# A residual block on one core: another order of the last pair of gate columns, earlier loads for the attention stage, and the meta tokens' probabilities transposed first

## The chip, the core and the metric

The kernel runs on one core of one Trainium2 chip. Its engines are PE (TensorE, the matrix unit), DVE (VectorE), ACT (ScalarE), POOL (GpSimd) and SP, which here only issues DMAs. Each engine works through its own instructions strictly in the order in which they were written, and waits for the others by semaphores. DMAs are issued from two queues: SP's (the weights) and POOL's (most stores and loads of activations, between POOL's own arithmetic). The metric is the device time of one execution in microseconds (us), from the first to the last instruction with what lies around it.

## The reference

One layer over 512 tokens and 16 prepended meta tokens (528 rows), width 2048, all in float32:

```
h = rmsnorm(r, mix_pre_g)
z = h @ w_in + b_in                    # q | k | v | forget logits | pool input u | g_attn | g_pool
c = cumsum(log_sigmoid(f_logit))       # per head
s = q @ k.T * 128**-0.5 + c[q] - c[k]  # causal, 8 heads of 128
attn = softmax(s) @ v
d = trailing_mean(u, windows 2,4,8,16) - u
pool = (d @ pool_w per group) * pool_scale
m = sigmoid(g_attn) * (attn @ w_attn_o) + sigmoid(g_pool) * (pool @ w_pool_o)
r = r + rmsnorm(m @ w_out, mix_post_g)
h = rmsnorm(r, ffn_pre_g)
a = causal_dwconv3(h @ w_ffn_up)
r = r + rmsnorm((gelu(gate(a)) * val(a)) @ w_ffn_down, ffn_post_g)
out = r[16:]
```

## The kernel before

Activations are kept transposed, 128 features in the partitions and the 528 tokens along the free axis. Every float32 product is made of three matmuls in the fast float32r format: both operands are split into a high part (a cast on ACT, line 292 or 193) and a low part (a subtraction on DVE, line 293 or 201), and `mm3` (line 303) adds high*high, high*low and low*high in PSUM.

**Input projection.** After four single columns the other 60 column blocks of `w_in` go through in pairs, in the order of `xpairs`. A pair is one step of Strassen's scheme (`strassen`): seven products of 24 matmuls each instead of eight. Its left factors are halves of the weights ("11", "12", "22") and sums of them ("S1" to "S4"); its right factors are blocks of x ("11", "21", "22", held in the tiles `xb`, `xh`, `xl`) and sums of them ("T1" to "T4", held in `ht`, `lt`). Products add up in the PSUM banks `pua`, `pub`, `puc`; ACT copies them out (lines 491 to 505) and DVE adds them. The list `units` (line 134) says in which order the weights' halves and sums are prepared, some three units ahead of PE.

**Work in the background.** `side` and `side2` hold generators. After each k of `mm3` they get a tick of that k's matmul time, and when the time that a generator asked for with `yield` is over, its next piece is written into the program there. So the background's place in the program is set by the amount of matmul work, not by what has finished. The output of a pair (`x_out`) goes this way: multiply by `rstd` on DVE (line 574), bias or sigmoid on ACT (line 578), store to DRAM from POOL (line 582).

**Between the pairs and the next projections.** The pool differences d come back from DRAM into eight tiles (`d_loads`, line 595, on SP's queue), are split into `dh` and `dl`, and `pool_out` multiplies them with the pool weights: four groups g, two outputs each, 24 matmuls a group, into the banks `py`, copied out as `yh` (ACT, line 796) and `yl` (DVE, line 797). After group 0, `forget_columns` loads the cumulated forget values (`fc`, line 469) and transposes them on PE (`pc`, line 472), and `head_loads` loads q, k and v of heads 0 and 1.

**po and attention.** Sixteen blocks of the pool's output projection follow (`half_proj`, banks `ppo`, 48 matmuls each); their results are multiplied by the gates (line 844) and stored (line 845). During them two lanes run in the background: lane 0 has heads 0, 2, 4, 6, lane 1 has heads 1, 3, 5, 7. For a head, `head_parts` splits q and k, transposes v (`pv`, `pvm`) and makes the products of the last two meta queries (`p2`, line 669). `attention` then goes through four blocks of 128 queries (i = 3, 2, 1, 0): bias row `dd` from the broadcast forget row `crow` (ACT, line 685), mask (POOL, line 686), scores `ps` (PE, line 691), then `s`, maximum, exponential (lines 695 to 699). Then the probabilities are transposed, key block by key block (`pt`, line 716, j = 3, 2, 1, 0) and split into `pth` and `ptl`; the 16 meta keys' probabilities are transposed last (`pm`, line 731) and split into `pmh`; and `pa` (line 742) multiplies with v: first the meta tokens, then j = 0, 1, 2, 3. At the end of lane 1 stand the meta tokens' own queries (`meta_queries`, lines 748 to 775). After that the attention's output projection (`pao`) begins.

All F tiles (activations) share one pool of 63 buffers that are handed out again when the last reader of a tile has run; PSUM has eight banks (tag "s") that go round, so a new bank waits for the copy-out of the tile that held it. The DMAs of POOL's queue use eight semaphores in turn; a DMA that takes one up again waits until the DMA that had it has landed.

Of the kernel before, what the change touches and what calls it, by code (L numbers as in the profile page):

```python
# [23 lines left out]
F32 = mybir.dt.float32  # L24
# [25 lines left out]
H = 8  # L50
# [24 lines left out]
def block(ctx, tc, xT, win, wf, wao, wpw, wpo, wout, wup, wdn, consts, out):  # L75
# [50 lines left out]

    loads, units, base = [], [], []
    for key in order:
        base.append(len(units))
        if key[0] == "pair":  # L130
            at0 = len(loads)
            for src in key[1:]:
                loads += [(srcs[src[0]](src[1]), c) for c in (0, 1024)]
            units += [(i, at0) for i in ("11", "12", "S2", "S1", "S3", "S4", "22")]
        else:
            for c in (0, 1024):
                units.append(("", len(loads)))
                loads.append((srcs[key[0]](*key[1:]), c))
# [29 lines left out]
    def make_source():  # L168
        i = at["sum"]
        kind, n = units[i]  # L170
        if kind == "":
            sources[i] = raw_of(n)
        else:
            a11, a12, a21, a22 = (raw_of(n + j) for j in range(4))
            if kind == "S2":
                for name in ("S1", "S2"):
                    sums[name] = wp.tile([P, 1024], F32, name="wsum", tag="wsum", bufs=2)
                dve.tensor_tensor(sums["S1"], a21, a22, op=OP.add)
                dve.tensor_tensor(sums["S2"], sums["S1"], a11, op=OP.subtract)  # L179
            elif kind == "S3":  # L180
                dve.tensor_tensor(a21, a11, a21, op=OP.subtract)
                drop(n)
            elif kind == "S4":
                dve.tensor_tensor(a12, a12, sums["S2"], op=OP.subtract)  # L184
            sources[i] = {"11": a11, "12": a12, "S3": a21, "S4": a12, "22": a22}.get(kind) or sums[kind]
# [281 lines left out]
    def forget_columns():  # L467
        cur = F("fc")[:H]
        nc.gpsimd.dma_start(cur, c_dram)
# [9 lines left out]
    def strassen(keys, blocks, n, skip=0, late=None):  # L479
# [26 lines left out]
        dve.tensor_tensor(gr, gr, c[:, skip:], op=OP.add)  # L506
        return zg, zv
# [91 lines left out]
    ds = []  # L599
# [20 lines left out]
    for ma, mb in xpairs:  # L620
        last = (ma, mb) == xpairs[-1]
# [52 lines left out]
    def attention(h, then=None):  # L674
# [36 lines left out]

        pth = [None] * 4
# [88 lines left out]
    for j, t in enumerate(ds):  # L801
        dh[j], dl[j] = F("dh", F32R), F("dl", F32R)
        split(t[:, T0:], dh[j][:, T0:], dl[j][:, T0:])
    ds.clear()

    def lane(n):
        if n:
            yield 8.0
# [19 lines left out]
    sg = {}  # L828
# [8 lines left out]
    for j in range(KT):  # L837
# [7 lines left out]
        nc.gpsimd.dma_start(po_dram[j][:, T0:], t[:, T0:])  # L845
    side.finish()
# [4 lines left out]
    pl = {}  # L851

    def sum_load(j):
        if j < KT:
            gate_load(j)
            pl[j] = F("pl")
            nc.gpsimd.dma_start(pl[j][:, T0:], po_dram[j][:, T0:])

    sum_load(0)
    sum_load(1)  # L860
# [354 lines left out]
```

## Time and profile before

| | |
|---|---|
| runs of the kernel before | median 2671.09 us of 3 (2663.85 to 2672.19) |
| the profiled execution | 2668.45 us, of which the span from the first to the last instruction is 2666.6 us |
| busy in the span | PE 96%, PE weight loads 92%, DVE 73%, ACT 45%, POOL 9% |
| PE's mean granted clock | 0.981 of full speed |

The share of busy time is a mean over stages with different limits. "PEclk" in a window is the granted clock: 1.00 is the upper of its two levels, 0.50 the lower, and values between are a mixture of the two in that window. A matmul's duration overlaps with the next, so PE's busy time has no gap where matmuls follow each other.

### The profile page before, as it was taken

The page shows a single profiled execution, that of the slowest core. Times are in us where ns is not written, and L with a number is a line of the kernel's source. Part 1 is how long each engine was busy: PE and PEld are TensorE (multiplying, and loading weights), DVE is VectorE, ACT ScalarE, POOL GpSimd, SP SyncE. Part 2 cuts the span into 40 slices and gives each one's busy share as a digit, 9 for nine tenths or more (in the row PEclk, how much of TensorE's full clock was granted, in tenths as well). Part 3 has the DMA queues.
Part 4 walks back from the last instruction along what each step waited for, and adds up shares of the span by engine and source line. Part 5 has one row for each costly group of instructions (what it writes and reads, how often), then busy time and mean ns, then how long its engine had stood idle before and what let it go on. Part 6 is the DMA issues. An engine that isn't in the chain of part 4 may idle for free.

```text
span 2666.6 us, 46374 instructions
## 1 busy us (share of the span) xinstructions
PE 2558.5 (96%) x18949; PEld 2450.8 (92%) x18949; DVE 1937.9 (73%) x2542; ACT 1210.7 (45%) x1851; POOL 227.2 (9%) x369
## 2 busy tenths in 40 slices
PE   8899999999888999999899999999999999999995
PEld 7899999999878899999899999999999978888885
DVE  8887778778766653489798888888888844545456
ACT  5544444444544423455555555455555542222232
POOL 3000000000122210034000000000000000000003
PEclk9999999999998999999999999999999999999997
DMA  4333433343543453578753333333333343333323
GB/s 165 104 121 135 139 125 122 134 143 121 200 141 113 137 179 99 181 243 274 225 182 125 110 115 124 119 107 123 127 108 119 125 155 113 122 116 122 114 90 127
DMA packets 129269, 369.57 MB, mean 139 GB/s; under 512 B 15758, under 2 KB 42128, under 8 KB 129056
## 3 DMA queue, kind: packets, MB, share of 16 engines
q1 hardware_dynamic: 112064, 310.48, 35.7%
q0 software_dynamic: 16992, 56.14, 5.7%
q8 instruction: 148, 2.42, 0.4%
q14 instruction: 65, 0.53, 0.1%
HBM read 319.34 MB, written 47.21 MB: 137 GB/s over the span
## 4 chain that ended last, share of the span: by engine, by line
PE 82%; DVE 7%; issue 6%; DMA 2%; ACT 2%; POOL 1%; SPq 0%; POOLq 0%; DVEq 0%; ACTq 0%
PE pua L303 28%; PE pd L303 18%; PE puc L303 14%; PE pub L303 7%; PE pw L303 6%; PE pu L303 4%; PE pao L303 3%; DVE wlo L201 1%; PE ppo L303 1%; PE pa L742 1%; DMA t<-h_dram 1%; ACT whi L193 1%; DVE xb L370 0%; DVE xr L543 0%; DVE lt L524 0%
## 5 line engine op out<-in xcount | busy, mean ns | idle before, releaser
L201 DVE TENSOR_TENSOR wlo<-wraw,whi 128x1024 fp32r<-128x1024 f32 x566 | 696.8, 1235 | 216.9 <-ACT whi L193 216.7
L193 ACT CAST whi<-wraw 128x1024 fp32r<-128x1024 f32 x566 | 594.3, 1051 | 517.6 <-DVE wraw L184 176.4
L303 PE MATMUL pua<-lt,whi 128*128 128x258 f32 (+1 forms) x1632 | 464.1, 284 | 0.0
L303 PE MATMUL pua<-h,whi 128*128 128x258 f32 x1520 | 371.0, 284 | 5.1 <-ACT z L491 5.1
L303 PE MATMUL pua<-h,wlo 128*128 128x258 f32 x1216 | 344.4, 283 | 0.0
L303 PEld LDWEIGHTS pua<-lt,whi 128*128 128x128 f32 x1632 | 309.9, 190 | 0.0
L303 PEld LDWEIGHTS pua<-h,whi 128*128 128x128 f32 x1520 | 267.4, 190 | 5.3 <-ACT z L491 5.3
L193 ACT CAST whi<-wsum 128x1024 fp32r<-128x1024 f32 x136 | 142.9, 1051 | 255.8 <-DVE wsum L179 251.7
L303 PE MATMUL pd<-fl,whi 128*128 128x512 f32 x640 | 252.1, 394 | 1.1 <-DVE fl L293 1.1
L303 PE MATMUL pd<-fh,wlo 128*128 128x512 f32 x640 | 251.7, 393 | 0.0
L303 PE MATMUL pd<-fh,whi 128*128 128x512 f32 x640 | 251.2, 393 | 0.0
L303 PEld LDWEIGHTS pua<-h,wlo 128*128 128x128 f32 x1216 | 231.4, 190 | 0.0
L1072 DVE TENSOR_TENSOR yacc<-yacc,pd 128x512 f32<-128x512 f32 x144 | 98.8, 686 | 167.6 <-PE pd L303 167.5
L303 PE MATMUL pua<-ht,whi 128*128 128x264 f32 x720 | 206.0, 286 | 12.2 <-ACT z L491 10.1
L303 PE MATMUL pua<-ht,wlo 128*128 128x264 f32 x720 | 205.2, 285 | 0.0
L201 DVE TENSOR_TENSOR wlo<-wsum,whi 128x1024 fp32r<-128x1024 f32 x136 | 166.0, 1222 | 53.9 <-ACT whi L193 53.9
L303 PE MATMUL puc<-h,whi 128*128 128x258 f32 x912 | 196.2, 282 | 0.0
L303 PE MATMUL puc<-h,wlo 128*128 128x258 f32 x608 | 171.4, 282 | 0.0
L303 PE MATMUL puc<-lt,whi 128*128 128x258 f32 (+1 forms) x544 | 153.9, 283 | 0.0
L303 PEld LDWEIGHTS puc<-h,whi 128*128 128x128 f32 x912 | 151.3, 189 | 0.0
L303 PEld LDWEIGHTS pua<-ht,whi 128*128 128x128 f32 x720 | 136.4, 189 | 12.8 <-ACT z L491 10.3
L303 PEld LDWEIGHTS pd<-fl,whi 128*128 128x128 f32 x640 | 120.1, 188 | 30.2 <-DVE fl L293 2.3
(326 smaller groups left out, 6305.4 us busy)
## 6 DMA issues: line engine op xcount, KB each, us to landing
wraw<-wup SPq DMA_DIRECT2D x200, 512.0 KB, 3.8
wraw<-win SPq DMA_DIRECT2D x128, 512.0 KB, 4.0
wraw<-wdn SPq DMA_DIRECT2D x88, 512.0 KB, 3.6
wraw<-wout SPq DMA_DIRECT2D x56, 512.0 KB, 4.4
act_dram<-cv POOLq DMA_DIRECT2D x44, 256.0 KB, 5.0
y<-act_dram SPq DMA_DIRECT2D x44, 256.0 KB, 4.9
sig_dram<-z POOLq DMA_DIRECT2D x32, 264.0 KB, 4.5
sg<-sig_dram POOLq DMA_DIRECT2D x32, 264.0 KB, 4.2
```

Source lines behind the costliest of these rows:

```text
L193: act.copy(ready[i][0], sources[i])
L201: dve.tensor_tensor(lo, sources.pop(i), f32(ready[i][0]), op=OP.subtract)
L303: pe.matmul(po, a, b[:, xs], start=k == 0 and j == 0 and not more, stop=k == nk - 1 and j == 2, skip_group_check=more)
L742: pe.matmul(pa[:, q0:], u, w, start=n == 0 and j == 0, stop=n == 4 and j == 2)
L1072: dve.tensor_tensor(yacc[i], yacc[i], ps, op=OP.add)
```

## The change

- The last pair takes a new function, `strassen_early`, and its weights the order EARLY. The three products that read x itself (right factors "21", "11", "22") come first, the four that read the sums after them. It uses a fourth PSUM bank (`pud`) and no `snap` copy; products five and six (T3, T4) both add to `pua`.
- A generator `prefetch` takes the place of `d_loads`: after the third product it loads `fc`, the eight d tiles and q, k, v of heads 0 and 1, all from POOL's queue.
- The d tiles are split four ahead of group 0, two after group 0, and two after group 1. Head 0's parts are added to the background after group 0 instead of group 2, and lane 1 begins after 4.0 us of matmul time instead of 8.0.
- The pairs' loop now stands behind the definitions of the attention; the output of the last pair is written out in the background's flush behind the first four d splits.
- In `attention` the meta keys are transposed and split first, ahead of the four key blocks, and `pa` takes the meta tokens, then j = 3, 2, 1, 0.
- The first two loads of the po results (`sum_load`) are issued within the po loop.

```
+    LATE = ("11", "12", "S2", "S1", "S3", "S4", "22")
+    EARLY = ("12", "11", "S4", "S2", "S1", "S3", "22")
...
-            units += [(i, at0) for i in ("11", "12", "S2", "S1", "S3", "S4", "22")]
+            early = key == ("pair", ("in", xpairs[-1][0]), ("in", xpairs[-1][1]))
+            units += [(i, at0) for i in (EARLY if early else LATE)]
...
-    def forget_columns():
-        cur = F("fc")[:H]
-        nc.gpsimd.dma_start(cur, c_dram)
+    def forget_columns(cur):
...
+    def strassen_early(keys, blocks, n, late):
+
+        unit = pair_weights(*keys)
+        a, b, c, d = (s_ps(x)[:, :n] for x in ("pua", "pub", "puc", "pud"))
+        zg, zv = F("z"), F("z")
...
+        gl, gr, vl, vr = zg[:, :n], zg[:, n:2 * n], zv[:, :n], zv[:, n:2 * n]
+        product(0, b, "21")
+        product(1, a, "11")
+        act.copy(gl, a)
+        product(2, d, "22")
+        side.add(late)
+        dve.tensor_tensor(gl, gl, b, op=OP.add)
+        product(3, a, "T2", True)
+        act.copy(gr, a)
+        product(4, c, "T1")
+        dve.tensor_tensor(gr, gr, d, op=OP.add)
+        product(5, a, "T3", True)
+        act.copy(vr, a)
+        dve.tensor_tensor(gr, gr, c, op=OP.add)
+        product(6, a, "T4", True)
+        act.copy(vl, a)
+        dve.tensor_tensor(vr, vr, c, op=OP.add)
+        return zg, zv
...
-    def d_loads():
-        for j in range(8):
-            t = F("d")
-            nc.sync.dma_start(t[:, T0:], d_dram[j][:, T0:])
-            ds.append(t)
-        yield 0.1
...
-        za, zb = strassen((("in", ma), ("in", mb)), XBLOCKS, XN, late=d_loads() if last else None)
-        side.add(x_out((ma, za), (mb, zb)))
-    side.finish()
-    side2.finish()
...
+        pm = s_ps("pm")
+        for i in range(4):
+            pe.transpose(pm[:META, P * i:P * (i + 1)], probs[i][0][:, :META], ident)
+        m = wp.tile([P, 1024], F32R, name="pmh", tag="wsum", bufs=2)[:META]
+        split(pm[:META], m[:, :512], m[:, 512:])
+        yield 1.2
         pth = [None] * 4
         for j in (3, 2, 1, 0):
...
-        pm = s_ps("pm")
-        for i in range(4):
-            pe.transpose(pm[:META, P * i:P * (i + 1)], probs[i][0][:, :META], ident)
-        m = wp.tile([P, 1024], F32R, name="pmh", tag="wsum", bufs=2)[:META]
-        split(pm[:META], m[:, :512], m[:, 512:])
-        yield 2.5
+        yield 1.3
...
-        for j in range(4):
+        for j in (3, 2, 1, 0):
             c = slice(P * j, P * (j + 1))
             steps.append((vh[:, c], vl[:, c], *pth[j], min(P * j, 256)))
...
+    def prefetch():
+
+        ds.append(F("fc"))
+        nc.gpsimd.dma_start(ds[0][:H], c_dram)
+        for j in range(8):
+            ds.append(F("d"))
+            nc.gpsimd.dma_start(ds[-1][:, T0:], d_dram[j][:, T0:])
+        head_loads(0)
+        head_loads(1)
+        yield 0.1
...
+        if last:
+            za, zb = strassen_early(keys, XBLOCKS, XN, prefetch())
...
+        if last:
+            side.finish()
+            side2.finish()
+        side.add(x_out((ma, za), (mb, zb)))
...
+    for j in range(4):
+        d_split(j)
+    side.finish()
...
-            yield 8.0
+            yield 4.0
...
         if g == 0:
-            forget_columns()
-            head_loads(0)
-            head_loads(1)
-        if g == 2:
+            forget_columns(fc)
+            del fc
             side.add(head_parts(0))
+        if g < 2:
+            d_split(2 * g + 4)
+            d_split(2 * g + 5)
...
+        if j == KT - 2:
+            sum_load(0)
+            sum_load(1)
```

On POOL, around the end of the last pair, the order of issues was this before (`sig_dram<-z` are the stores of the gates, `sg` the gates' loads for po):

```order
L582 DMA sig_dram<-z 128x528 x8
L469 DMA fc<-c_dram 8x528
L646 DMA qkv<-qkv_dram 128x528 x6
L833 DMA sg<-sig_dram 128x528 x2
L634 DMA crow<-c_dram 128x528
L646 DMA qkv<-qkv_dram 128x528 x3
L686 AFFINE_SELECT dd<-dd 128x128 x2
L833 DMA sg<-sig_dram 128x528
L845 DMA po_dram<-sg 128x514
L634 DMA crow<-c_dram 128x528 x2
```

And now:

```order
L611 DMA sig_dram<-z 128x528 x6
L819 DMA fc<-c_dram 8x528
L822 DMA d<-d_dram 128x514 x8
L660 DMA qkv<-qkv_dram 128x528 x6
L611 DMA sig_dram<-z 128x528 x2
L648 DMA crow<-c_dram 128x528
L885 DMA sg<-sig_dram 128x528 x2
L700 AFFINE_SELECT dd<-dd 128x128 x4
L885 DMA sg<-sig_dram 128x528
L897 DMA po_dram<-sg 128x514
L648 DMA crow<-c_dram 128x528
```

The fifteen loads have moved ahead of the last pair's own two stores, the d loads came over from SP's queue, and heads 1 and 2 no longer have their `crow` loads together behind the second po store: head 1's stands behind the first.

On ACT, at the end of the last pair, before:

```order
L505 COPY z<-pua 128x264
L578 ACTIVATE z<-z,cs 128x528 x2
L292 CAST dh<-d 128x514 x8
L796 ACTIVATE yh<-py,cs 128x258
L796 ACTIVATE yh<-py,cs 128x256
```

And now:

```order
L534 COPY z<-pua 128x264
L295 CAST dh<-d 128x514 x4
L607 ACTIVATE z<-z,cs 128x528 x2
L811 ACTIVATE yh<-py,cs 128x258
L811 ACTIVATE yh<-py,cs 128x256
L295 CAST dh<-d 128x514 x2
L295 CAST qh<-qkv 128x528
L295 CAST vh<-pv 128x512
L295 CAST vmh<-pvm 16x128
```

Four splits of d now come ahead of the last pair's output, and its two activations stand between them and the copies out of group 0; head 0's parts stand between the copies out of group 0 and those of group 1.

On PE, in head 0 (rows of `ppo` and `ps` between them are left out here), before:

```order
L716 MATMUL pt<-ident,s 128x128 x4
L731 MATMUL pm<-ident,s 16x128 x4
L742 MATMUL pa<-pmh,vmh 128x512 x2
L742 MATMUL pa<-pth,vh 128x512
L742 MATMUL pa<-pth,vh 128x384
L742 MATMUL pa<-pth,vh 128x256 x2
```

And now:

```order
L728 MATMUL pm<-ident,s 16x128 x4
L736 MATMUL pt<-ident,s 128x128
L736 MATMUL pt<-ident,s 128x128 x4
L757 MATMUL pa<-pmh,vmh 128x512 x2
L757 MATMUL pa<-pth,vh 128x256 x2
L757 MATMUL pa<-pth,vh 128x384
L757 MATMUL pa<-pth,vh 128x512
```

The transposes of the meta keys have moved ahead of all those of the key blocks, and within `pa` the block that is transposed last (j = 0, 512 columns) is now the last to be read.

## Rows read from the trace of the kernel before

**Rows 1.** Windows of 100 and 50 us: each engine's busy time, granted clock, DMA share.

```profile
core 0: us, PE busy (x) PEld busy (x) DVE busy (x) ACT busy (x) POOL busy (x), PEclk, DMA share, GB/s
500.00:600.00 100.00, 100.00 (x822) 100.00 (x821) 78.65 (x87) 49.68 (x70) 5.42 (x10) 1.00 0.39 132
700.00:750.00 50.00, 41.10 (x318) 39.95 (x317) 33.60 (x71) 31.40 (x62) 11.98 (x23) 0.93 0.63 223
750.00:800.00 50.00, 39.88 (x267) 36.00 (x267) 32.01 (x84) 19.78 (x47) 13.91 (x32) 0.91 0.49 150
800.00:850.00 50.00, 45.92 (x308) 42.70 (x307) 33.22 (x84) 23.36 (x55) 12.38 (x31) 0.88 0.43 128
850.00:900.00 50.00, 44.73 (x310) 40.47 (x309) 33.67 (x85) 23.07 (x55) 8.72 (x23) 0.93 0.24 77
```

**Rows 2.** PE's waits, 640 to 960 us: total, times, longest.

```profile
PE ppo L303 <- DVE s L695: 4.8, 2, 3.6
PE pa L742 <- DVE pmh L293: 4.8, 7, 1.2
PE pc L472 <- DMA fc<-c_dram: 4.1, 1, 4.1
PE p L669 <- DVE vl L293: 4.0, 3, 2.1
PE pa L742 <- ACT pmh L292: 3.3, 4, 1.4
PE py L303 <- ACT dh L292: 2.5, 1, 2.5
PE ps L691 <- DVE pth L293: 1.4, 1, 1.4
...
PE pua L303 <- ACT z L496: 0.8, 1, 0.8
PE pt L766 <- DVE s L758: 0.7, 1, 0.7
...
PE pa L775 <- DVE vm L772: 0.4, 1, 0.4
```

**Rows 3.** Windows of 5 us, same columns as Rows 1.

```profile
715.00:720.00 5.00, 2.06 (x12) 2.02 (x13) 2.57 (x7) 2.71 (x6) 2.62 (x5) 0.62 1.03 413
...
815.00:820.00 5.00, 4.85 (x15) 3.91 (x16) 3.89 (x13) 1.44 (x3) 2.72 (x5) 0.52 0.42 124
```

**Rows 4.** Timeline of PE: start, us, line, operation, out<-in, idle before and its releaser.

```profile
814.31 0.50 PE L742 MATMUL pa<-pmh,vmh 16*128 16x512 f32 x1 [1.13 <-ACT pmh L292]
```

**Rows 5.** Timeline of ACT and DVE, 707 to 720 us.

```profile
707.76 0.38 ACT L505 COPY z<-pua 128x264 f32<-128x264 f32 x1 [2.02 <-PE pua L303]
708.11 1.53 ACT L578 ACTIVATE z<-z,cs 128x528 f32<-128x528 f32 x2
...
711.74 2.59 ACT L292 CAST dh<-d 128x514 fp32r<-128x514 f32 x4 [0.81 <-DMA d<-d_dram]
...
707.37 1.51 DVE L574 TENSOR_TENSOR z<-z,rstd 128x528 f32<-128x528 f32 x2
...
712.39 2.66 DVE L293 TENSOR_TENSOR dl<-d,dh 128x514 fp32r<-128x514 f32 x4 [0.74 <-ACT dh L292]
```

**Rows 6.** Timeline of POOL's and SP's queues: start, us, operation, count, idle before.

```profile
701.22 0.54 POOL L582 DMA_DIRECT2D sig_dram<-z  x1 [2.37 <-ACT z L578]
...
710.47 0.52 POOL L469 DMA_DIRECT2D fc<-c_dram  x1
...
752.60 0.55 POOL L845 DMA_DIRECT2D po_dram<-sg  x1 [7.63 <-DVE sg L844]
...
705.05 4.10 SPq L595 DMA_DIRECT2D d<-d_dram  x8
```

**Rows 7.** Tile qkv: time from issue to landing of its loads.

```profile
DMA to landing us min/median/max: 3.1/6.0/8.2
```

**Rows 8.** The chain of waits, 640 to 960 us: start, us, what.

```profile
771.71 2.85 PE pa L742 x14
```

More of the change, by code (lines that the diff above doesn't have):

```diff
@@ L174, in make_source @@
             a11, a12, a21, a22 = (raw_of(n + j) for j in range(4))
-            if kind == "S2":
+            if kind in ("S2", "S4") and (n, "S2") not in sums:
                 for name in ("S1", "S2"):
[L177 to L180, printed above, removed]
+                    sums[n, name] = wp.tile([P, 1024], F32, name="wsum", tag="wsum", bufs=2)
+                dve.tensor_tensor(sums[n, "S1"], a21, a22, op=OP.add)
+                dve.tensor_tensor(sums[n, "S2"], sums[n, "S1"], a11, op=OP.subtract)
+            if kind == "S3":
                 dve.tensor_tensor(a21, a11, a21, op=OP.subtract)
@@ L183, in make_source @@
             elif kind == "S4":
-                dve.tensor_tensor(a12, a12, sums["S2"], op=OP.subtract)
-            sources[i] = {"11": a11, "12": a12, "S3": a21, "S4": a12, "22": a22}.get(kind) or sums[kind]
+                dve.tensor_tensor(a12, a12, sums[n, "S2"], op=OP.subtract)
+            sources[i] = {"11": a11, "12": a12, "S3": a21, "S4": a12, "22": a22}.get(kind) or sums[n, kind]
         at["sum"] += 1
@@ L506, in strassen, with product @@
         dve.tensor_tensor(gr, gr, c[:, skip:], op=OP.add)
+        return zg, zv
[3 more added lines that the diff above has]
+        zg, zv = F("z"), F("z")
+        def product(i, ps, block, more=False):
+            mm3([(ps, slice(0, n))], HK, unit(i), blocks[block], more)
+        gl, gr, vl, vr = zg[:, :n], zg[:, n:2 * n], zv[:, :n], zv[:, n:2 * n]
[15 more added lines that the diff above has]
+        dve.tensor_tensor(vr, vr, c, op=OP.add)
         return zg, zv
@@ L590, in x_evac @@
         side.add(x_out((m, z), scaled=True))
-    def d_loads():
-        for j in range(8):
-            t = F("d")
-            nc.sync.dma_start(t[:, T0:], d_dram[j][:, T0:])
-            ds.append(t)
-        yield 0.1
-    ds = []
     XBLOCKS = {"11": lambda k: xb[0, k], "21": lambda k: xb[0, HK + k], "22": lambda k: xb[1, HK + k]}
@@ L619, in block @@
     side2.add(forget())
-    for ma, mb in xpairs:
-        last = (ma, mb) == xpairs[-1]
-        za, zb = strassen((("in", ma), ("in", mb)), XBLOCKS, XN, late=d_loads() if last else None)
-        side.add(x_out((ma, za), (mb, zb)))
-    side.finish()
-    side2.finish()
     vmeta = cp.tile([P, H, META], F32, name="vmeta")
@@ L799, in pool_out, with d_split @@
             yl.append(lo)
-    for j, t in enumerate(ds):
-        dh[j], dl[j] = F("dh", F32R), F("dl", F32R)
-        split(t[:, T0:], dh[j][:, T0:], dl[j][:, T0:])
-    ds.clear()
+    def prefetch():
[7 more added lines that the diff above has]
+        yield 0.1
+    ds = []
+    for ma, mb in xpairs:
+        last = (ma, mb) == xpairs[-1]
+        keys = ("in", ma), ("in", mb)
+        if last:
+            za, zb = strassen_early(keys, XBLOCKS, XN, prefetch())
+        else:
+            za, zb = strassen(keys, XBLOCKS, XN)
+        if last:
+            side.finish()
+            side2.finish()
+        side.add(x_out((ma, za), (mb, zb)))
+    fc = ds.pop(0)[:H]
+    def d_split(j):
+        dh[j], dl[j] = F("dh", F32R), F("dl", F32R)
+        split(ds[j][:, T0:], dh[j][:, T0:], dl[j][:, T0:])
+        ds[j] = None
+    for j in range(4):
+        d_split(j)
+    side.finish()
     def lane(n):
         if n:
-            yield 8.0
+            yield 4.0
             yield from head_parts(n)
@@ L827, in block, with sum_load @@
     po_dram = dp.tile([KT, P, L], F32, name="po_dram")
-    sg = {}
+    sg, pl = {}, {}
+    def sum_load(j):
+        if j < KT:
+            gate_load(j)
+            pl[j] = F("pl")
+            nc.gpsimd.dma_start(pl[j][:, T0:], po_dram[j][:, T0:])
     def gate_load(n):
@@ L850, in block @@
     mh, ml = [], []
[L851 to L860, printed above, removed]
     for j in range(KT):
```

## The prediction

> **What bounds the kernel now.** I read the windows first, to see where PE is not full. Over most of the program PE is busy without a gap at full clock, 822 matmuls in 100 us, or 0.122 us each; in the stretch from 700 to 900 us, pool projection and attention, it is busy 41 + 40 + 46 + 45 of 200 us and its clock is 0.93, 0.91, 0.88, 0.93 [rows 1]. Elsewhere in the program this change alters nothing on PE, so its whole worth must come from this stretch. It loses time in two ways. PE stands still for 28.4 us in the four windows [rows 1]. And it runs at the lower of its two clock levels: a window at clock c has (1 - c) / 0.5 of its time at half pace, so 7 + 9 + 12 + 7 = 35 us [rows 1]. Half of that, 17.5 us, is lost if PE has work all through; it has not in the window from 715 us, where it is busy 2.06 of 5 us, so I count 14 us.
>
> Next, PE's waits say what for. In groups: the start of the pool projection 6.6 us (2.5 for the first split of d, 4.1 for the forget row fc); `pa` for the split of the meta keys 8.1 us (4.8 + 3.3); `ppo` and `ps` at the start of the attention lanes for `s` and `pth` 6.2 us (4.8 + 1.4); the meta queries' product `p2` for the split of v 4.0 us; the end of lane 1 1.1 us (0.7 + 0.4) [rows 2]. DVE and ACT are no bound here: DVE is busy about 33 of each 50 us, ACT 20 to 31 [rows 1]. These are latencies of chains across engines. Last, where the low clock sits: 0.62 in the window in which PE waits for fc, and 0.52 in the one from 815 us, in which PE gets through 15 matmuls [rows 3] and which begins with `pa` behind a wait of 1.13 us for the split of the meta keys [rows 4].
>
> **The change part by part.** The terms are made against the profiled execution, 2668.45 us; the median of the three runs is 2.6 us above it.
>
> *Order of the last pair.* The same 168 matmuls. New is that T4 adds to `pua` right behind T3, with ACT's copy out between them, so PE waits for that copy. The trace has a wait of this kind, `pua` for the copy of line 496: 0.8 us [rows 2]; I take **+0.8**, between 0.5 (the copy alone is 0.38 [rows 5]) and 1.9 (a weight cast ahead of it on ACT). One ACT copy is dropped, one DVE add is added, and the weight sum S4 is needed one product after its operands; that lies under a product's 24 x 0.122 = 2.9 us, several of which are prepared ahead: 0.
>
> *First split of d.* Before, PE waited 2.5 us for `dh`, since ACT did the last copy, then two activations of 1.53 us in all [rows 5], and the d loads could only be issued from 705.05 us, behind weight loads on SP's queue [rows 6]. Now the prefetch stands behind the store of the pair before, issued at 701.22 us [rows 6], and each issue takes 0.54, so the first d is asked for at about 702.3, 2.8 us earlier, and ACT goes from the last copy straight to the split. What is late next: copy 0.38, one split 2.59 / 4 = 0.65, some 0.2 between, then 0.5 of the low part (2.66 / 4 = 0.67, PE has two matmuls meanwhile) [rows 5]: 1.7 against 2.5. **-0.8**; from -2 to +2 if d lands late.
>
> *fc.* It was issued at 710.47 [rows 6], now some 8.6 us earlier and ahead of the other loads. Even with the DMA engines as full as they were then (share 1.03 [rows 3]) that is more than twice the wait. **-4.1**, and 0 to lose.
>
> *New waits within the pool projection.* Head 0's parts now sit in group 1. `pv` takes the bank of the first `py`, which is free when DVE has made `yl`. PE gets there 24 + 5 + 6 matmuls after the first `py`, 4.3 us. ACT and DVE first finish four d splits (DVE 2.66), then DVE multiplies the last pair's output by rstd (1.51), ACT does its second activation (0.75), then `yh` and `yl`, some 0.45 each [rows 5]: 5.8 us. So 1.5 us of wait, 0.4 more for `pvm`. In group 2 the same again, a bank behind the split of v (0.7), and a bank behind `yl` and a weight split (0.5). Together 3.1, **+3.0**. The lower bound is 0. For the upper, q, k and v must have landed: v of head 0 is the third load behind the d loads, asked for at about 709.5, and these loads took 3.1 to 8.2 us [rows 7], so it lands up to 717.7 against PE at about 715: up to +5.5.
>
> *The meta keys first.* Between `pm` and the first `pa` matmul stood some 18 matmuls of `ppo`, 18 x 0.122 = 2.2 us, and the waits of 8.1 us over eight heads say that this was 1 us too little on average. Now `pmh` is ready four transposes earlier. What is late next is `ptl` of block j = 0. Its distance to `pa` is again 12 to 18 matmuls, but `pa` reads it last: behind twelve matmuls at 2.85 / 14 = 0.20 us [rows 8], 2.4 us more. That is more than the mean wait of 1.0 and about the longest sum of one head (1.4 + 1.2 [rows 2]). **-7.5**, from -8.1 to -4 (half of it back where DVE is late).
>
> *Start of the lanes.* `ppo` waited 3.6 us because head 1's `crow` load stood on POOL behind the second po store, which had itself waited 7.63 us for DVE [rows 6]. It now stands behind the first. But the load itself still has to land before DVE can go on, so I take **-2.0** of the 5.0 (3.6 + 1.4); from -5 to 0. `p2` still waits for the split of v as before: **0**.
>
> *End.* The meta queries now have po matmuls beside them: **-1.1**. The early po result loads save nothing, as PE has no wait for them.
>
> *Clock.* Of the 35 us at half pace, the stretches behind `pa` waits are about half; the pool projection's may return, since its new waits sum to nearly what the old were. Of 14 us lost I take a third, **-5.0**, from -14 to 0.
>
> Sum: 0.8 - 0.8 - 4.1 + 3.0 - 7.5 - 2.0 - 1.1 - 5.0 = -16.7, so 2668.45 - 16.7 = 2651.75; I forecast 2651.8.
>
> **The rivals.**
> *The clock stays low.* The long waits are cut up into short ones at bank changes, and the half-pace time stays at 35 us. For it: the window at 0.52 follows a wait of 1.13 us, and no wait of `pa` is longer than 1.4 [rows 2 to 4]. Against it: their number falls. Without the clock term 2668.45 - 11.7 = 2656.8. The Trainium skill ("TensorE: Matmul & The Clock Gate", section "A second HAM failure mode: psum-queue depth-cycling") says that a PE which idles briefly and often between groups of matmuls, as PSUM banks are cycled, swings between its two clock levels though no single pause is long. By that rule this rival would hold; the trace agrees in so far as that low window follows a short wait.
> *The waits only move.* With eight banks and DVE in order, `pa` then waits for block 0 or the next bank instead: 2 of the 8.1 are gained, start and clock give nothing: 0.8 - 0.8 - 4.1 + 3.0 - 2.0 - 1.1 = -4.2, 2664.2. For it: `ppo` and `pvm` already wait for DVE today. Against: DVE is a third idle.
> *All of it comes.* No new waits in the pool projection, the start's 5.0, `pa`'s 8.1 and the clock's 14: 0.8 - 0.8 - 4.1 - 8.1 - 5.0 - 1.1 - 14 = -32.3, 2636.2.
> *Slower, by POOL's queue.* Each later head's `crow` and q, k, v loads come to stand behind a po store that waits for DVE, as head 1's did. Each such head costs 3.6 + 1.4 and a stretch at half pace, some 2.7: 7.7 us. From three heads on it eats the gain; with four, and the start's 2.0 not gained, 2651.8 + 31 + 2 = 2685. For it: the queue is in order and now carries eight loads more. Against: these eight are over before po begins, and before only one head was hit.
>
> **How the numbers follow.** Forecast 0.51, clock stays low 0.17, all of it 0.10, waits only move 0.14, slower 0.08. A difference under 0.3%, 8 us, cannot be told from none. The first three are faster by more: 0.78. Waits that only move are within it: 0.14. Slower: 0.08. The likeliest case alone spans 2642 to 2660 (the clock term by 5 either way, the `pa` and pool terms by 3 each). The range goes from 2637, next to the case in which all comes, to 2667, past that in which waits move; outside are the slower case and about a half of the full gain.
>
> **What would show it.** PE's wait for fc gone; first `py` within 1.5 us of the last pair's end; PE's waits for `pmh` under 1 us in all and none of more than 1 us for `ptl` of block 0; a new wait of `pv` or `pvm` for `yl` of 1 to 2 us; `pao` beginning some 17 us earlier, with the program behind it unchanged; the stretch's half-pace time about 25 us. The prediction is wrong if the clock falls in the pool projection for longer than before, if `pv` waits for its load well past 718 us, or if `crow` is late for more than one head.

## The result and the profile after

The changed kernel took 2652.94 us, median of 4 runs (2649.82 to 2655.38), against 2669.00 us, median of 4, for the kernel before: ratio 0.9939, 95% interval 0.9926 to 0.9952, 16.1 us less. Forecast were 2651.8 us in a range of 2637 to 2667. The profiled execution took 2654.53 us, span 2652.8 us.

The same windows of the changed kernel as in [rows 1] (us; each engine's busy time with its instructions; granted clock; DMA share; GB/s):

```profile
500.00:600.00 100.00, 100.00 (x822) 100.00 (x821) 80.30 (x88) 48.33 (x68) 5.04 (x10) 1.00 0.37 125
700.00:750.00 50.00, 43.00 (x325) 41.57 (x324) 35.99 (x78) 31.31 (x62) 17.78 (x35) 0.93 0.64 222
750.00:800.00 50.00, 44.85 (x316) 40.87 (x315) 34.62 (x89) 24.80 (x57) 13.53 (x34) 0.93 0.50 159
800.00:850.00 50.00, 47.28 (x335) 43.15 (x336) 39.13 (x104) 26.19 (x62) 12.97 (x32) 0.97 0.42 130
850.00:900.00 50.00, 45.54 (x345) 42.13 (x344) 31.46 (x77) 20.75 (x46) 8.29 (x23) 1.00 0.35 111
```

In the window from 500 us, ahead of the stretch, nothing has changed: 822 matmuls, as before. Inside the stretch PE's busy time has gone from 171.6 to 180.7 of 200 us, and the time at half pace, (1 - clock) / 0.5 of each window, from 35 to 7 + 7 + 3 + 0 = 17 us.

The stage can be cut out of the trace by PE's own first rows: from the first matmul of the last pair to the first `pao`. Before, it ran from 687.07 to 921.64, 234.57 us; after, from 689.14 to 906.98, 217.84 us. These are the first `pao` rows of before and of after (start, us, what, idle before):

```profile
921.64 0.51 PE L303 MATMUL pao<-ah,whi 128*128 128x258 f32 x2 [0.25 <-ACT ah L292]
```
```profile
906.98 0.51 PE L306 MATMUL pao<-ah,whi 128*128 128x258 f32 x2 [0.25 <-ACT ah L295]
```

So the stage is 16.73 us shorter. The program ahead of it took 2.07 us longer and the program behind it 0.86 us (1744.96 and 1745.82 us to the end of the span), so the two profiled executions differ by 13.8 us in all. By the first `ppo` matmul the stage divides into the pair with the pool projection, 42.64 before and 40.65 after (-1.99), and the lanes, 191.93 and 177.19 (-14.74). PE's idle times in its timeline add up to 29.55 us before (28 of them) and 19.12 after (21); the other 6.3 us are time in which PE works, now with about half as much of it at half pace.

PE's waits after, 640 to 960 us (total, times, longest), which answer to [rows 2]:

```profile
PE pt L736 <- DVE pmh L296: 3.5, 3, 1.6
PE pv L674 <- DMA qkv<-qkv_dram: 2.9, 1, 2.9
PE pvm L677 <- DVE vl L296: 2.4, 1, 2.4
PE ps L705 <- DVE s L709: 1.6, 1, 1.6
PE pm L728 <- DVE s L653: 1.5, 1, 1.5
PE pv L674 <- DVE ptl L296: 1.2, 1, 1.2
PE py L306 <- ACT dh L295: 1.0, 1, 1.0
PE pa L757 <- ACT pth L295: 0.9, 1, 0.9
...
PE pa L757 <- DVE ptl L296: 0.7, 2, 0.5
PE ppo L306 <- DVE pmh L296: 0.7, 1, 0.7
```

The wait for `fc` is gone, and `pa`, which waited 8.1 us for the meta keys, waits 0.9 + 0.7. New are `pt` behind `pmh` (a transpose that needs a PSUM bank which DVE has not yet read), `pv` behind its own load, and `pvm` behind the split of `v`.

### The profile page after: what moved, and what is told of

The parts are those of the page before. It is cut to its first block, busy times and chain, and to the rows that moved or that the text cites. A ratio compares the mean times of both kernels' runs of the same rounds, so it can differ in the third digit from the quotient of the medians.

```text
span 2652.8 us, 46370 instructions
## 1 busy us (share of the span) xinstructions
PE 2555.4 (96%) x18949; PEld 2447.4 (92%) x18949; DVE 1934.3 (73%) x2543; ACT 1209.4 (46%) x1850; POOL 230.1 (9%) x377
## 4 chain that ended last, share of the span: by engine, by line
PE 61%; DVE 3%; issue 3%; DMA 2%; POOL 1%; ACT 1%; SPq 0%; POOLq 0%; DVEq 0%; ACTq 0%
PE pd L306 18%; PE pua L306 16%; PE puc L306 8%; PE pw L306 6%; PE pub L306 4%; PE pao L306 3%; PE pu L306 3%; PE ppo L306 1%; DVE wlo L204 1%; PE pa L757 0%; DMA t<-h_dram 0%; DMA x<-xT 0%; POOL mix L973 0%; PE ps_rs L324 0%; DVE mix L969 0%
## 5 line engine op out<-in xcount | busy, mean ns | idle before, releaser
L306 PEld LDWEIGHTS pua<-ht,whi 128*128 128x128 f32 x720 | 136.6, 190 | 12.9 <-ACT z L492 10.4
```

The lines of the kernel that those rows point to most:

```text
L306: pe.matmul(po, a, b[:, xs], start=k == 0 and j == 0 and not more, stop=k == nk - 1 and j == 2, skip_group_check=more)
```

## The experiments

All medians, with the range of the runs, the ratio to the kernel before on the same chip, and the stage in one profiled execution each (first matmul of the last pair to first `ppo`; first `ppo` to first `pao`). In the first column "loads" is the new order of the last pair with the earlier loads, "meta" the meta keys first, "lane 4" the odd lane at a pace of 4 instead of 8.

| kernel | us (runs) | ratio [95%] | pool part | lanes |
|---|---|---|---|---|
| before | 2667.8 to 2669.0 in five sets | | 42.6 | 191.9 |
| lane 4 | 2675.0 (2672.7 to 2678.0) | 1.0029 [1.0018, 1.0040] | 41.4 | 199.5 |
| meta | 2658.1 (2656.4 to 2660.4) | 0.9962 [0.9950, 0.9975] | 41.6 | 182.6 |
| loads | 2659.4 (2656.4 to 2661.7) | 0.9971 [0.9960, 0.9981] | 40.4 | 184.1 |
| meta + lane 4 | 2660.8 (2656.2 to 2662.2) | 0.9972 [0.9963, 0.9981] | 43.1 | 183.2 |
| loads + lane 4 | 2662.2 (2660.8 to 2665.4) | 0.9974 [0.9965, 0.9984] | 40.6 | 190.7 |
| loads + meta | 2659.5 (2656.1 to 2660.6) | 0.9963 [0.9951, 0.9976] | 41.2 | 183.6 |
| all three (the change), again | 2653.6 (2650.4 to 2656.9) | 0.9951 [0.9938, 0.9963] | 41.7 | 178.8 |
| change, odd lane at 2 | 2656.3 (2654.0 to 2656.6) | 0.9952 [0.9939, 0.9964] | 40.7 | 179.1 |
| change, old order of the pair | 2649.6 (2646.8 to 2650.5) | 0.9928 [0.9915, 0.9940] | 40.7 | 177.5 |
| change, head 0 ahead of d4 | 2647.0 (2646.2 to 2648.9) | 0.9928 [0.9915, 0.9940] | 38.9 | 178.2 |
| that, old order of the pair | 2648.4 (2644.6 to 2649.2) | 0.9921 [0.9907, 0.9934] | 38.5 | 177.7 |
| that, head 1's `crow` early | 2648.7 (2645.9 to 2649.0) | 0.9923 [0.9909, 0.9936] | 39.1 | 176.7 |

How far single executions scatter: the changed kernel's two profiles have 217.84 and 220.49 us in the stage.

### The parts of the change, one at a time and in pairs

**Meta first, alone.** `pm` and its split ahead of the four blocks, and the accumulation turned round, in the kernel before:

```diff
+        pm = s_ps("pm")
...
+        yield 1.2
         pth = [None] * 4
         for j in (3, 2, 1, 0):
...
-        yield 2.5
+        yield 1.3
         pa = s_ps("pa")
...
-        for j in range(4):
+        for j in (3, 2, 1, 0):
```

> The kernel before with one part of the change: the meta tokens' probabilities are transposed, copied and subtracted ahead of the four key blocks instead of behind them, and the output's accumulation goes m, 3, 2, 1, 0 instead of m, 0, 1, 2, 3. Theory (the prediction's own term): the 14 waits of the output for ACT's and DVE's copies, 8.1 us in all, go nearly whole, so 7.5 us less than before and a little clock with it: about 2660 us, the stage from the first matmul of the last pair to the first one of the attention projection 8 to 10 us shorter. Rival (the waits only move: transposes of the blocks wait for PSUM banks behind the meta tokens' split, as 3.5 us of pt's waits in the changed kernel hint): 0 to 2 us less, about 2668 us, and the gain of the whole change lies in the earlier loads.

2658.1 us, 10.7 us less than before; the stage is 10.4 us shorter, 9.3 of them in the lanes. The theory has the number, and `pa`'s waits go as it said: 8.1 us before, 0.4 now. But the rival is right about the waits: 5.6 us of waits for `pmh` have come up at other places, and these are the three largest (PE's waits of this kernel; total, times, longest):

```profile
PE ps L691 <- DVE pmh L293: 2.2, 1, 2.2
PE pvm L663 <- DVE pmh L293: 1.6, 1, 1.6
PE pt L722 <- DVE pmh L293: 1.3, 1, 1.3
```

PE's idle time in the lanes is 20.7 us, against 22.8 before, so only 2.0 of the 9.3 us are idle time. The other 7.3 are time in which PE works, at a mean granted clock of 0.96 over the lanes instead of 0.93. Why the clock was higher is not shown.

**All but the meta keys.** The same lines put back in the changed kernel.

> The changed kernel with the meta tokens' probabilities put back behind the four blocks and the old order of the output's accumulation; the new order of the last pair, the early loads and the start of the lanes stay. Theory: the output waits again as it did, 7 to 8 us, so 2660 us, about half of the change's 16 us; fc's wait stays away. Rival (waits only move): 2653 to 2655 us, no measurable difference from the changed kernel.

2662.2 us, 9.3 us above the first set of the changed kernel and 8.6 above the second. `pa`'s waits are back, 15.1 us in four groups, of which these two are the largest (PE's waits of this kernel, total, times, longest):

```profile
PE pa L756 <- ACT pmh L295: 8.2, 4, 3.3
PE pa L756 <- DVE pmh L296: 5.1, 7, 1.8
```

**The odd lane at 8 again.** In the changed kernel:

```diff
-            yield 4.0
+            yield 8.0
             yield from head_parts(n)
```

> The changed kernel with the odd heads' lane starting after a pace of 8 instead of 4 (as before). Theory (the prediction's term for the start of the lanes, which gave it 2.0 us): the second lane's first head comes later and the first half of the first two projection blocks has less work to put between its waits: 1 to 3 us more, 2654 to 2656 us. Rival: the first waits of the odd lane (2.4 us for the split of v, 1.6 us for s) come from its starting too early, while its row of c still loads behind the first store of the pool projection; with 8 they are hidden and the time is 1 to 3 us less, 2650 to 2652 us.

2659.5 us: 6 to 7 us lost, more than either theory gave to this one number. The rows show a wait that neither the kernel before nor the changed one has, that of the meta queries' product `p` (L683) for ACT's copy of k. PE's waits (total, times, longest), and PE's and ACT's timelines at one of the three places:

```profile
PE p L683 <- ACT kh L295: 8.5, 3, 4.0
```
```profile
819.23 0.60 PE L674 MATMUL pv<-ident,qkv 128*128 128x128 f32 x4
823.16 0.38 PE L683 MATMUL p<-kh,qh 128*128 128x256 f32 x1 [3.22 <-ACT kh L295]
```
```profile
821.44 0.52 ACT L713 ACTIVATE s<-s,st 128x272 f32<-128x272 f32 x1 [1.97 <-DVE st L652]
821.87 0.19 ACT L713 ACTIVATION_READ_ACCUMULATOR s<-s,st 128x1 f32 x1
821.96 0.61 ACT L295 CAST qh<-qkv 128x528 fp32r<-128x528 f32 x1
822.48 0.63 ACT L295 CAST kh<-qkv 128x528 fp32r<-128x528 f32 x1
```

The next head's q and k were there, but in ACT's order their split stands behind the other lane's exponential, and this waited 1.97 us for DVE's `st` (the row names line 652, a reciprocal; the maximum of these scores, lines 711 and 712, ends just before it). PE has passed `pv` at 819.23 and stands before the meta queries' product until 823.16. The wait is set by which lane's work is ahead of which in an in-order engine.

**The loads alone** (the changed kernel with meta last and the odd lane at 8), **meta first with lane 4** (the kernel before with these two edits), and **lane 4 alone**:

> The changed kernel with the meta tokens last again and the odd lane starting after a pace of 8 again: what is left of the change are the order of the last pair and the earlier loads. Theory (the prediction's terms for these: fc 4.1 and the first split 0.8 us less, T4's wait 0.8 and the wait of v's transposes 3.0 us more, a microsecond or so of clock): about 2667 us, 1 to 3 us less than before. Rival (each part simply adds: with meta first and the odd lane at 4 worth 9.3 and 6.6 us, nothing is left for the loads): 2669 us, as before. A second rival (the loads carry the gain, since they let the lanes begin 10 us earlier): 2660 us or less.

> The kernel before with two parts of the change, the meta tokens first and the odd lane at a pace of 4, with the old order and the old loads. Theory: the gain in the stage of the lanes doesn't need the earlier loads, so all of the change but the 2 us by which its pool projection ended sooner: 2654 to 2656 us. Rival: the early start of the odd lane pays only once its q, k and v are there; with the old loads its first head waits for them, and the time stays at the 2658 us of the meta tokens alone, or above.

> The kernel before with one part of the change, the odd lane starting after a pace of 4 instead of 8; it completes the eight combinations of earlier loads, meta tokens first and odd lane at 4. Theory (the pace only sets how the lanes stand to each other; with one of the other two parts alone it cost 2.7 and 2.8 us, and it paid 6.3 us only where both were there): no gain, 2668 to 2672 us. Rival (the prediction's own term for the start of the lanes, 2.0 us from work that lies beside the first projection blocks): 2666 us or less.

2659.4, 2660.8 and 2675.0 us. The loads alone are worth 8.4 us where the theory had 1 to 3; the second rival had the number, though by the profile only 2.2 us lie in the pool part and 7.8 in the lanes, whose code is the old one there. Meta first with lane 4 came out above meta first alone, on the rival's side, though not by its cause: no wait for q, k or v is in the rows, and ACT's one wait for a row of `c` is 3.1 us, 3.7 in the changed kernel. And lane 4 alone gains nothing, as the theory had it, but it costs 7.1 us, with `pa` standing longer than before (PE's waits):

```profile
PE pa L742 <- ACT pmh L292: 11.7, 4, 4.8
```

The eight combinations are far from additive. Meta first gives 10.7 alone, 14.2 with lane 4, 0 with the loads (2659.4 and 2659.5), and 8.6 to 9.3 with both. Lane 4 costs 7.1, 2.7 and 2.8, and gives 6 to 7 where both others are there. These are medians from several chips; by the ratios, each to the kernel before on its own chip, meta first gives 10, 15, 2 and 6 to 9, and lane 4 costs 8, 3 and 1 and gives 3 to 6. So the costs of 2.7 and 2.8 us, the 0 and the exact size of the last gain lie within the noise; the large differences do not.

What differs between them in the trace is the step of the two lanes: the time from the first score matmul of one head to that of the next. Here are heads 0 to 3 of the kernel with loads and meta first, and of the changed kernel (PE's timeline):

```profile
730.55 0.40 PE L705 MATMUL ps<-kh,qh 128*128 128x264 f32 x2
751.83 0.40 PE L705 MATMUL ps<-kh,qh 128*128 128x264 f32 x2
763.29 0.41 PE L705 MATMUL ps<-kh,qh 128*128 128x264 f32 x2
796.98 0.40 PE L705 MATMUL ps<-kh,qh 128*128 128x264 f32 x2
```
```profile
730.51 0.40 PE L705 MATMUL ps<-kh,qh 128*128 128x264 f32 x2
748.02 0.41 PE L705 MATMUL ps<-kh,qh 128*128 128x264 f32 x2
770.26 0.64 PE L705 MATMUL ps<-kh,qh 128*128 128x264 f32 x2
790.62 0.40 PE L705 MATMUL ps<-kh,qh 128*128 128x264 f32 x2
```

The first goes 21, 11, 34, then on to the end 10, 33, 10, 32: its heads run in close couples. The second goes 18, 22, 20, 18, 22, 16, 23. The loads alone have the steps of the first (10 and 31 to 32 from head 2 on), loads with lane 4 those of the second (17 to 23). So where heads go in couples, the place of the meta keys makes no difference, because `pa` hardly waits there in either form (0.3 and 1.2 us for them and for `ptl` when they are last), and PE loses its time at the meta queries' product instead, 9.7 and 8.5 us for ACT's `kh`. Where heads alternate evenly, `pa` waits 13.3 us for the meta keys if they come last and not if they come first. Lane 4 alone starts head 1 only 10.0 us behind head 0 and head 2 33.5 us later, but goes on in steps of 17 to 26; there `pa` waits 14.3 us for the meta keys, and meta first, with steps of 10, 32, 18, 24, 14, 27 and 18, gives the most.

That the step causes the waits is read from these rows and from their going together in these kernels; no run moved the step alone and kept everything else. The next one changes it once more.

**The odd lane at a pace of 2**, in the changed kernel:

> The changed kernel with the odd lane starting after a pace of 2 instead of 4. Theory (what the pace sets is the step between the lanes, not how early the odd one is done: which lane's copies stand ahead of the other's in ACT's and VectorE's order): no steady gain, anything between 2652 and 2660 us, with other waits in the rows. Rival (the earlier the odd lane starts, the more of the lanes' work lies beside projection blocks, 6.3 us for the step from 8 to 4): 2649 to 2651 us.

2656.3 us, with steps of 14, 26, 18, 22, 18, 22, 16. Earlier is not better: 8, 4 and 2 gave medians of 2659.5, 2653.6 and 2656.3, and by the ratios 4 and 2 are the same (0.9951 and 0.9952). This is the theory's side.

### The loads and the order of the last pair

**Old order of the last pair, early loads kept:**

```diff
-            units += [(i, at0) for i in (EARLY if early else LATE)]
+            units += [(i, at0) for i in LATE]
...
-            za, zb = strassen_early(keys, XBLOCKS, XN, prefetch())
+            za, zb = strassen(keys, XBLOCKS, XN, late=prefetch())
```

> The changed kernel with the last pair multiplied in the order of all other pairs (11, 12, S2, S1, S3, S4, 22) and the same early loads. Theory: x's 11 and 22 blocks and the raw weights stay in use longer, so the loads of d, issued in order behind one another, wait for their buffers; the last of them and the six loads of q, k and v behind them land 4 to 8 us later, and the first transposes of v and the second half of the pool projection wait for them: 3 to 6 us more than the changed kernel, 2656 to 2659 us. Rival (the order only costs, by its wait of T4 for ACT's copy, 0.5 us; the loads have slack): 2652 to 2653 us, as the changed kernel or a little below.

2649.6 us; the theory fell. The first load of `d` is issued 15.2 us after the pair's first matmul in both. With the old order the pair ends 0.74 us sooner, and so does the first `py` start; by the first `ppo` both stand at 40.7 us, since `pv` now waits longer, and for VectorE's low part of d instead of the load:

```profile
PE pv L674 <- DVE dl L296: 3.7, 1, 3.7
```

The new order bought nothing here. Whether it costs the 3 to 4 us by which the medians differ is less sure, since the stages of the profiles do not show it (218.2 against 217.8 and 220.5).

**The changed kernel once more**, as a control:

> The changed kernel once more, as the control beside which variants are read: its four runs so far lay between 2649.8 and 2655.4 us, and the variant with the old order of the last pair 3 us lower although its stage up to the attention projection was not shorter (218.2 us against 217.8). If the order of the last pair is neutral, this control comes out near 2650 us too; if the order costs something that the one profile didn't show, it stays at 2653.

2653.6 us: it stays where it was, though the intervals of the ratios overlap (0.9938 to 0.9963, and 0.9915 to 0.9940 with the old order). The profiles place most of the difference outside the stage. Against the first profile of the changed kernel, the one with the old order is 4.9 us shorter in its span: 1.9 us ahead of the stage and 3.4 behind it, while the stage is 0.3 longer; against the second profile it is 7.2 us shorter, 2.3 of them in the stage. Most of what lies behind it is in the pairs of the FFN's up projection, the same code in both kernels. Here is the time from their first matmul to the first of the down projection, of the changed kernel and of the one with the old order (columns as above):

```profile
1348.61:2126.08 777.47, 772.34 (x6386) 772.13 (x6385) 666.08 (x737) 404.04 (x578) 21.05 (x39) 1.00 0.36 120
```
```profile
1346.37:2121.04 774.67, 769.54 (x6386) 769.33 (x6385) 665.65 (x737) 404.54 (x578) 21.06 (x39) 1.00 0.37 120
```

The same 6386 matmuls take 2.8 us longer in the changed kernel, at the same granted clock: in windows of 10 us it is below 1.00 only in the first two, 0.96 and 0.69 there and 0.99 and 0.67 with the old order. The second profile of the changed kernel has 777.47 us too; the kernel before has 775.9. Why they do is not shown, so it is not shown either that the order of the last pair costs anything.

**Head 0's loads ahead of d4.** The new wait of `pv` was for a load. POOL's queue in the changed kernel shows why the load came late (start, us, operation, idle before):

```profile
703.83 0.52 POOL L819 DMA_DIRECT2D fc<-c_dram  x1
704.35 3.21 POOL L822 DMA_DIRECT2D d<-d_dram  x6
708.64 0.54 POOL L822 DMA_DIRECT2D d<-d_dram  x1 [1.08 <-PE pua L306]
709.77 0.54 POOL L822 DMA_DIRECT2D d<-d_dram  x1 [0.60 <-PE pua L306]
710.30 1.18 POOL L660 DMA_DIRECT2D qkv<-qkv_dram  x2
712.24 0.54 POOL L660 DMA_DIRECT2D qkv<-qkv_dram  x1 [0.77 <-DMA d<-d_dram]
```

Head 0's `v`, the third load of `qkv`, is issued at 712.24, behind two loads of `d` that waited for buffers of the last pair. `pv` needed it at 716.4:

```profile
719.31 0.83 PE L674 MATMUL pv<-ident,qkv 128*128 128x128 f32 x4 [2.92 <-DMA qkv<-qkv_dram]
```

The edit:

```diff
             nc.gpsimd.dma_start(ds[-1][:, T0:], d_dram[j][:, T0:])
-        head_loads(0)
+            if j == 3:
+                head_loads(0)
         head_loads(1)
```

> The changed kernel with the loads of head 0's q, k and v ahead of the last four blocks of d. Theory (the wait of v's first transpose, 2.9 us for the load of v, is real): it goes, and the second half of the pool projection, whose d now comes 2 us later, waits 0 to 1.5 us: 1.5 to 3 us less, 2650 to 2651 us where the control has 2653. Rival (with the load there, the same transpose waits 2.5 to 4 us for VectorE's subtractions of d and q instead, as it did with the old order of the last pair): no difference from the control.

2647.0 us, 6.6 us below the control beside it, with no run in common: the theory's side, but more than the wait itself. The pool part is 1.8 to 2.8 us shorter, the whole stage 0.7 and 3.4 us (217.1 against 217.8 and 220.5). The spans of the profiles differ by 6.7 and 9.0 us; 4.4 and 5.2 of these lie behind the first `pao`, where the code is the same. So most of the gain is not placed in what the edit moved, and its cause is open. In the wait's place stands a smaller one, for `yl`:

```profile
PE pv L674 <- DVE yl L812: 1.3, 1, 1.3
```

And the clock stays up behind it. Windows of 5 us around the `pv` wait of the changed kernel, and of this one (columns as above):

```profile
715.00:720.00 5.00, 2.08 (x18) 1.74 (x17) 3.77 (x10) 4.76 (x10) 3.01 (x6) 0.96 1.02 401
720.00:725.00 5.00, 5.00 (x32) 5.00 (x31) 3.81 (x10) 3.09 (x9) 1.85 (x4) 0.70 0.99 361
```
```profile
713.00:718.00 5.00, 3.75 (x33) 3.35 (x32) 3.77 (x11) 4.28 (x9) 3.08 (x6) 1.00 1.02 390
718.00:723.00 5.00, 4.87 (x39) 4.46 (x37) 5.00 (x12) 5.00 (x12) 2.33 (x5) 1.00 0.95 330
```

Behind 2.92 us of standing still the clock is at 0.70; behind 1.25 us it is at 1.00. (The length of the wait does not decide this, as the last run below shows.) From 700 to 900 us the four windows of this kernel have 0.97, 0.97, 1.00 and 1.00, 6 us at half pace instead of 17. The second profile of the changed kernel has 13, and the one with the odd lane at 2, which took 2656.3 us, has 6 as well, so this does not make up the 6.6 us. Here are the first two of the four:

```profile
700.00:750.00 50.00, 41.77 (x320) 39.49 (x318) 35.09 (x78) 31.28 (x62) 17.60 (x36) 0.97 0.69 238
750.00:800.00 50.00, 45.01 (x323) 41.23 (x324) 35.98 (x93) 24.65 (x59) 13.41 (x34) 0.97 0.45 138
```

**Two things more on top of it**, the old order of the last pair, and head 1's row of `c` loaded behind head 1's q, k and v instead of behind the first store of the projection:

```diff
         head_loads(1)
+        crows[1] = crow_load(1)
         yield 0.1
...
-        heads[h] = parts, (vh, vl, vmh, vml), crow_load(h)
+        heads[h] = parts, (vh, vl, vmh, vml), crows.pop(h, None) or crow_load(h)
```

> The changed kernel with head 0's q, k and v loaded ahead of the last four blocks of d, and with the old order of the last pair. Theory (the new order only costs: T4's wait of 0.5 us and a first block of the projection that starts 0.7 us later, while the buffers that it frees early are not what the loads wait for longest): 2644 to 2646 us, 1 to 3 us below the same kernel with the new order (2647.0). Rival (with head 0's loads put forward, the raw weights and x's blocks that the old order holds on to delay d4 to d7, and the second half of the pool projection waits): 2648 us or more.

> The changed kernel with head 0's loads ahead of the last four blocks of d, and with head 1's row of c loaded behind head 1's q, k and v instead of behind the first store of the pool projection. Theory (the prediction's term for the start of the odd lane, with the wait that stands there: head 1's first row of dd waits 4.4 us for that load, and TensorE 2.4 us for s behind it): the wait goes, 2 to 3 us less than the 2647.0 without it, 2644 to 2645 us. Rival (the load shares the full queues of the pool projection, or the lanes only fall into another step with each other): 2647 us or more.

2648.4 and 2648.7 us: neither can be told from 2647.0. So the old order, 3 to 4 us better in the changed kernel, is no better here; the rival has the number but not the cause, since the pool part is not longer (38.5 us against 38.9). With the early `crow`, PE's wait of 2.4 us for `s` behind it is gone, and `pvm`'s wait for the split of `v`, a step earlier on the same lane, has grown from 2.4 to 3.3 us:

```profile
PE pvm L677 <- DVE vl L296: 3.3, 1, 3.3
```

So 0.9 of the 2.4 us have moved one place up the lane, which is the rival's side. And the clock fell behind the first `pv` wait, though this was only 1.32 us long, again for `yl`. In the windows in which the kernel with head 0's loads put forward has 1.00 twice, this one has:

```profile
713.00:718.00 5.00, 3.68 (x22) 3.47 (x23) 3.77 (x10) 5.00 (x11) 3.26 (x6) 0.77 1.02 394
718.00:723.00 5.00, 5.00 (x39) 5.00 (x39) 5.00 (x12) 4.60 (x10) 2.15 (x4) 0.89 0.94 318
```

The last four kernels of the table have ratios of 0.9921 to 0.9928, with intervals that overlap; no one of them is shown to be the fastest.

## Why the prediction was right

The number was right, 2651.8 against 2652.9, and so were most of its terms in size. The terms for waits add up to -11.7; PE's idle time in the stage fell by 10.4 us in one profile of the changed kernel and by 7.2 in the other. One term was wrong in kind, two came by another road than forecast, and the sum was made as if the terms were independent, which they are not.

*Order of the last pair, +0.8.* The pair lasts 0.73 us longer; PE's row at T4 has 0.47 us of wait for ACT's copy. The size was right. That the kernel with the old order came out 3 to 4 us lower was not foreseen, and by the profiles it does so mostly outside the stage.

*First split of d, -0.8.* Twice that: the first `py` comes 1.27 us behind the pair's last matmul instead of 2.77.

```profile
711.51 0.51 PE L306 MATMUL py<-dh,whi 128*128 128x258 f32 x2 [0.99 <-ACT dh L295]
```

*fc, -4.1.* The wait is gone. But 4.1 was one execution's: in the three experiments that kept the old load, the same wait was 2.3, 2.6 and 2.3 us. The term was too large by about 1.6.

*New waits within the pool projection, +3.0.* In place and size right (2.9 us at the first `pv`), in cause wrong: I put it to the bank behind `yl`, and had the late load of `v` only as the upper bound. Once the load is early, the waits for `yl` that I had worked out, 1.5 for `pv` and 0.5 for a later bank, appear: 1.25 for `pv` and 0.56 for a `py`. That d's and head 0's loads, issued from one queue or two, would share the same DMA engines is stated by the Trainium skill ("DMA: Bandwidth & Descriptors", section "Issuing engines are not separate DMA queues"); the trace has the engines full while `pv` waits (a DMA share of 1.02 at 401 GB/s), but no run here moved a load to another queue alone. What took this wait away was another order on one queue.

*The meta keys first, -7.5.* 10.7 us alone, so the size holds, the mechanism only in part. I had the waits vanish and the time with them. Alone, the part took 2.0 us of idle time out of the lanes and 7.3 us of working time at a higher mean clock; between the changed kernel and the one with the meta keys last, the profiles' lanes differ by 13.5 us, 6.8 of them idle time. Of what I listed as signs two failed: there was no wait for `yl` in the changed kernel, and PE still waits 4.2 us for `pmh` in all (3.5 in `pt`, 0.7 in `ppo`), no longer at `pa` but where a PSUM bank is still to be read. That is part of "the waits only move", and about half of what `pa` gave.

*Start of the lanes, -2.0.* This is the step that failed. I read the earlier start as an earlier place for one load, with nothing to lose; the bounds were 0 and -5. The pace costs 7.1 us alone, gains nothing beside one other part, and gives 6 to 7 us (3 to 6 by the ratios) only beside both. What it changes in the traces is how the two lanes stand to each other on ACT and DVE. The loads, too, gained mostly in the lanes (7.8 us of the profile's 10); I take it that this is the step again, since they start head 0's scores 3.2 us sooner behind the first `ppo` matmul (0.7 us instead of 3.9), but no run shows it.

*End, -1.1.* Right: before the first `pao` only its own 0.25 us are left.

*Clock, -5.0.* The half-pace time fell from 35 to 17 us, and to 13 in the second profile, where I expected 25; I put the 6.3 us of the stage's gain that are not idle time to this term (6.9 in the second profile).

Of the rivals, *the clock stays low* did not come. By the rule of the Trainium skill that stood beside it ("TensorE: Matmul & The Clock Gate", section "A second HAM failure mode: psum-queue depth-cycling") many short pauses at bank changes would have kept the clock swinging between its levels; the trace has pauses of `pt` behind a bank, 3 of up to 1.6 us, and half as much time at half pace. *The waits only move* came in part. *Slower by POOL's queue* did not: ACT waits for a row of `c` once, 3.7 us in head 1, and for no later head.

So the good total owes something to luck: the single parts (-10.7, -8.4, +7.1) sum to -12.0, and the whole gave 14 to 16 us.

## What to carry to other kernels

Where two chains are interleaved on in-order engines, a constant that sets when the second one starts is a parameter of its own: measure it again with every other edit, and read the time between the starts of the chains before pricing a wait, since the same edit was worth 0 or 14 us in kernels that differed only in the early loads and that constant, and the step went with it. Price a wait from several executions where the table of waits has it only once; one of 4.1 us was 2.3 to 2.6 in the others. When a load is put forward, write down everything issued ahead of it on its queue, and put first what is needed first: three lines that moved head 0's loads past four blocks shortened the pool part by 1.8 to 2.8 us. And before a difference of a few microseconds is put to an edit, compare the stretches whose code is the same: here what lies behind the first `pao` took 1740.0 to 1747.0 us in the profiles of the changed kernel and its variants.

## What was not expected of the hardware

The clock did not follow the length of a pause. In the 5 us from the end of the first `pv` wait PE's granted clock was 0.66 behind 2.92 us of waiting (the changed kernel) and 1.00 behind 1.25 us (head 0's loads put forward), but 0.66 again behind 1.32 us (head 1's `crow` early as well). Behind the wait of 2.49 us for the first split of d it was 1.00 in the kernel before and 0.66 in the one with meta first alone. So a wait can cost more than its length, and its length alone does not tell when.

The same 6386 matmuls of the FFN took 2.8 us more in one kernel than in another at the same granted clock; no row tells why.
